# Expert gating in a PEER layer: one-hot columns interleaved in twos, and one weighting operation for two float16 parts

## The chip, the cores and the metric

The kernel runs on one NeuronCore of a Trainium2 chip. The metric is the device time of one execution in microseconds (us). The engines are named as in the profile: PE (TensorE, matmuls; its weight loads are listed apart as PEld), DVE (VectorE), ACT (ScalarE), POOL (GpSimd) and SP (SyncE, which issues most transfers).

## The reference, cut to what matters

A token sequence of 256 positions and width 1024 runs through two layers with mixers and feed-forward parts and then through a third, hybrid layer, whose feed-forward part is a PEER layer: 8 heads each choose 16 of 128 x 128 = 16384 experts for every token. This is the part that the change touches:

```python
PEER_HEADS = 8; PEER_NKEYS = 128; PEER_EXPERTS = 128 * 128; PEER_TOPK = 16
qh = (xc @ w_q).reshape(Ct, H, 2, PEER_QDIM // 2)
s = jnp.einsum("nhad,akd->nhak", qh, sub_keys).astype(f32)
top_s, top_i = lax.top_k(s, K)
...
best_s, pos = lax.top_k(cand, K)
eidx = jnp.take_along_axis(cand_idx, pos, axis=-1)      # 128 * i + j
gate = jax.nn.softmax(best_s, axis=-1)
ug = u_tab[eidx]
vg = v_tab[eidx]
hpre = jnp.einsum("nd,nhkd->nhk", xc, ug).astype(f32)
act = (gate * jax.nn.gelu(hpre, approximate=False)).astype(x.dtype)
return jnp.einsum("nhk,nhkd->nd", act, vg)
```

## The kernel before

All weights stream from memory in blocks of 128 x 1024 float32, each issued by SP. `Stream._split` (lines 247 and 248) turns a block into two fp32r parts: ACT writes the rounded part `hi`, DVE the remainder `lo`. Every dense product is then three matmuls (hi by x-high, hi by x-low, lo by x-high).

The PEER layer doesn't gather experts. It computes gelu(x u) for all 16384 of them, in two halves of 64 rows i (`u_phase`, matmuls of 256 columns at lines 330 to 332), into `H[0]` and `H[1]`, whose partition is j and whose free axes are i and the token t. Then it multiplies H by a dense table of gates that is zero where an expert wasn't chosen, and multiplies the result by all of v (the v phase, matmuls of 512 columns at line 1343).

`routing` (line 1410) leaves, for every token, 128 choices (8 heads x 16) on the partitions: `ri` and `rj` hold the two halves of the expert's number in bfloat16, `rg` the gate scaled by 2^15 as two float16 parts (the rounded value at line 1529, the remainder at line 1530).

`gates` (line 1533) builds the table from these. It takes eight tokens at a time, 32 groups for each half of H, 64 in all. A group is
- on DVE: `oj` (line 1545), which compares `rj` with 0 to 127 and gives a one-hot row of 128 columns for each token; `oi` (line 1546), the same for `ri` and the 64 rows of this half; `gi` (line 1549), `oi` times the gate, one operation for each of the two float16 parts;
- on PE (line 1555): for each token two matmuls, one for each part, with `oj` of the token as the weights (128 x 128) and `gi` of the token as the moving operand (128 x 64), summed over the 128 choices into one PSUM bank for the eight tokens;
- on DVE (line 1558), one group later: H times that bank.

The four tokens of a half group lie side by side in the innermost axis of `oj`, `oi` and `gi`, and `iota` holds each of its numbers four times for the comparison. A token's columns, as the matmul reads them, are thus every fourth float16 element.

The gating group is a generator: the kernel's `pump` advances it between the blocks of the main loop by a credit. The groups of `H[0]` run during the second half of the u phase, those of `H[1]` during the first half of the v phase. `oj` and `gi` have two buffers each, `oi` has one.

Of the kernel before, what the change touches and what calls it, by code (L numbers as in the profile page):

```python
# [12 lines left out]
BF16 = mybir.dt.bfloat16  # L13
F16 = mybir.dt.float16
# [3 lines left out]
ALU = mybir.AluOpType  # L18
# [3 lines left out]
P = 128  # L22
T = 256
# [110 lines left out]
def _constants():  # L134

    f = np.float32
    parts = []

    def put(name, a):
        a = np.asarray(a, f).reshape(P, -1)  # L140
        CON[name] = (sum(p.shape[1] for p in parts), a.shape[1])
        parts.append(a)

    i = np.arange(P)
    r, c = i[:, None], i[None, :]
    put("ident", np.eye(P))
    inv = (f(10000.0) ** (-np.arange(32, dtype=f) / f(32))).astype(f)
    ang = (np.arange(T, dtype=f)[:, None] * inv[None, :]).astype(f)
    put("cos", np.tile(np.cos(ang).T, (4, 1)))
    put("sin", np.tile(np.sin(ang).T, (4, 1)))  # L150
    put("causal", np.concatenate([np.zeros((P, P)), np.where(c <= r, 0, BIG)], axis=1))
    put("sb_m01", r < c)
    put("sb_add", np.concatenate([np.where(r < c, 0, -BIG), np.zeros((P, P)), np.where(r < c, 0, -BIG)], axis=1))
    put("sb_tri", np.where(r >= c, -1, 0))
    put("sb_one", -np.ones((P, P)))
    lev = [np.where(r > c, 1, 0), np.where(r <= c, 1, 0)]
    msk = []
    for m in (64, 32, 16, 8, 4, 2, 1):
        blk = c // (2 * m)
        last = blk * 2 * m + m - 1  # L160
        second = (c % (2 * m)) >= m
        lev.append(np.where(second, (r > last) & (r <= c), (r > c) & (r <= last)))
        msk.append((r // (2 * m) == c // (2 * m)) & (r % (2 * m) < m) & (c % (2 * m) >= m))
    msk.append(r == c)
    put("hg_lev", np.concatenate(lev, axis=1))
    put("hg_msk", np.concatenate(msk, axis=1))
    slopes = [2.0 ** -(h + 1) for h in range(8)]
    ali = []
    for s in slopes:
        ali += [s * (P + r - c), np.where(c <= r, s * (r - c), BIG)]  # L170
    put("alibi", np.concatenate(ali, axis=1))
    cmp = []
    for tt in range(2):
        for s in slopes:
            d = (tt * P + r) - (16 * np.arange(32)[None, :] + 31)
            cmp.append(np.where((d >= 0) & (np.arange(32)[None, :] < 15), s * d, BIG))
    put("cmp_bias", np.concatenate(cmp, axis=1))
    put("cmp_row", np.stack([i >= 31, i >= 0], axis=1))
    put("iota_j", np.broadcast_to(np.repeat(np.arange(P), 4), (P, 4 * P)))
    put("iota16", np.broadcast_to(np.repeat(np.arange(16), 16), (P, 256)))  # L180
    starts = []
    for a0, a1, w in CAND:
        base = sum((y - x) * z for x, y, z in CAND if y <= a0)
        starts += [base + (a - a0) * w for a in range(a0, a1)]
    put("starts", np.broadcast_to(np.repeat(starts, 16), (P, 256)))
    put("dstarts", np.broadcast_to(np.repeat(np.diff([0] + starts), 16), (P, 256)))
    return np.concatenate(parts, axis=1)


def _arrays(inp):  # L190
    names, blocks = [], []
    for n, b in _weights(inp):
        names.append(n)
        blocks.append(b)
    w = np.stack(blocks)
    x = inp["x"][0].reshape(T, NK, P).transpose(2, 1, 0)
    sk = inp["peer_sub_keys_2"][0].transpose(0, 2, 1).reshape(P, P)
    pe = np.tile(inp["nsa_cmp_pe_2"][0].T, (2, 1))
    wc = np.stack([inp["nsa_w_cmp_k_2"][0], inp["nsa_w_cmp_v_2"][0]]).reshape(2, 2, 16, 64, 64).transpose(1, 3, 0, 2, 4)
    wc = wc.reshape(P, -1)  # L200
    arrays = {
        "w": w, "x": x, "vec": _vectors(inp), "con": _constants(),
        "sk": sk, "pe": pe, "wc": wc, "fin": inp["norm_final_2"].reshape(1, D),
    }
    return names, {k: np.ascontiguousarray(v, dtype=np.float32) for k, v in arrays.items()}
# [54 lines left out]
class K:  # L260
# [498 lines left out]
    def hybrid(self, acc):  # L759
        nc, tc = self.nc, self.tc  # L760
        xh, xl = (lambda k: self.xh[:, k]), (lambda k: self.xl[:, k])
        with ExitStack() as c:
# [106 lines left out]
            def gates():  # L869
# [4 lines left out]
                for h in range(4):  # L874
                    nc.vector.tensor_scalar(hgg[:, h], hgg[:, h], self.vec("hgn", h), None, ALU.mult)

            self.later(gates, 1.5)
            fill(self.both(lambda q: self.hgrn(q, hq, hk, hf, hg_i, hgg, ob["hg"]),
                           lambda q: self.nsa(q, ns_q, ns_k, ns_c, ns_v, gate, ob["nsa"])))
# [375 lines left out]
    def peer(self, acc):  # L1255
        nc, tc = self.nc, self.tc
        mm = nc.tensor.matmul
        HALF = P // 2
        with ExitStack() as c:
            pk = c.enter_context(tc.tile_pool(name="pk", bufs=1, reuse_waits="tile"))  # L1260

            ri = pk.tile([P, T], BF16, name="ri")
            rj = pk.tile([P, T], BF16, name="rj")
            rg = pk.tile([P, 2, T], F16, name="rg")
            iota = pk.tile([P, P, 4], BF16, name="iota")
            o = CON["iota_j"][0]
            nc.gpsimd.dma_start(iota, self.a["con"][:, o:o + 4 * P].rearrange("p (j t) -> p j t", t=4))
            H = [None, None]
            hp0 = c.enter_context(tc.tile_pool(name="h0", bufs=1, reuse_waits="tile"))
            H[0] = hp0.tile([P, HALF, T], F32, name="H0")  # L1270
# [16 lines left out]
            with ExitStack() as c2:  # L1287
# [9 lines left out]
                g = self.vec("ffn2")  # L1297
# [112 lines left out]
    def routing(self, rp, qT, sk, ri, rj, rg):  # L1410
        nc, tc = self.nc, self.tc
        mm = nc.tensor.matmul
        with ExitStack() as c:
            p = c.enter_context(tc.tile_pool(name="ro", bufs=1, reuse_waits="tile"))

            def table(name):
                t = p.tile([P, 16, 16], BF16, name="t_" + name)
                o = CON[name][0]
                nc.gpsimd.dma_start(t, self.a["con"][:, o:o + 256].rearrange("p (a s) -> p a s", s=16))
                return t  # L1420

            starts, dstarts, iota = table("starts"), table("dstarts"), table("iota16")
            rest = p.tile([P, P], F32, name="rest")
            rest2 = p.tile([P, NCAND], F32, name="rest2")
            for tt in range(2):
# [3 lines left out]
                for h4 in range(2):  # L1429
                    bs = [self.bank() for _ in range(2)]  # L1430
                    for h in range(4):
                        for a in range(2):
                            mm(bs[a][:, h * P:(h + 1) * P], qT[64 * a:64 * a + 64, 4 * h4 + h, tt * P:(tt + 1) * P], sk[64 * a:64 * a + 64],
                               start=h == 0, stop=True, skip_group_check=True, tile_position=(64 * a, 0))
# [14 lines left out]
                o = 0  # L1449
                for a0, a1, w in CAND:  # L1450
                    n = a1 - a0
# [68 lines left out]
                b = self.bank()  # L1520
                for n, t in enumerate((key[:, 0], key[:, 1], best)):
                    nc.tensor.transpose(b[:, n * P:(n + 1) * P], t.rearrange("p h s -> p (h s)"), self.ident)
                ts = slice(tt * P, (tt + 1) * P)
# [2 lines left out]

                g = p.tile([P, P], F32, name="g")
                nc.vector.tensor_scalar(g, b[:, 2 * P:3 * P], GSCALE, None, ALU.mult)
                nc.vector.tensor_copy(rg[:, 0, ts], g)
                nc.vector.tensor_tensor(rg[:, 1, ts], g, rg[:, 0, ts], ALU.subtract)  # L1530
                yield 3.5

    def gates(self, pool, H, half, ri, rj, rg, iota):

        nc = self.nc
        HALF = P // 2
        prev = None
        for t8 in range(T // 8 + 1):
            if t8 < T // 8:
                ts = slice(8 * t8, 8 * t8 + 8)  # L1540
                oj = pool.tile([P, 2, P, 4], F16, name="oj")
                oi = pool.tile([P, 2, HALF, 4], F16, name="oi", bufs=1)
                gi = pool.tile([P, 2, 2, HALF, 4], F16, name="gi")
                r4 = lambda t: t.rearrange("p (g t) -> p g t", t=4)[:, :, None, :]
                nc.vector.tensor_tensor(oj, iota[:, None].to_broadcast([P, 2, P, 4]), r4(rj[:, ts]).to_broadcast([P, 2, P, 4]), ALU.is_equal)
                nc.vector.tensor_tensor(oi, iota[:, None, half * HALF:(half + 1) * HALF].to_broadcast([P, 2, HALF, 4]),
                                        r4(ri[:, ts]).to_broadcast([P, 2, HALF, 4]), ALU.is_equal)
                for n in range(2):
                    nc.vector.tensor_tensor(gi[:, n], oi, r4(rg[:, n, ts]).to_broadcast([P, 2, HALF, 4]), ALU.mult)
            yield 1.5  # L1550
            if t8 < T // 8:
                b = self.bank().rearrange("p (t i) -> p t i", t=8)
                for t in range(8):
                    for n in range(2):
                        nc.tensor.matmul(b[:, t], oj[:, t // 4, :, t % 4], gi[:, n, t // 4, :, t % 4], start=t + n == 0, stop=n == 1, skip_group_check=True)  # L1555
            if prev is not None:
                pb, pt = prev
                nc.vector.scalar_tensor_tensor(H[:, :, pt], pb.rearrange("p t i -> p i t"), 1.0 / GSCALE, H[:, :, pt], ALU.mult, ALU.mult)  # L1558
            prev = (b, ts) if t8 < T // 8 else None
            yield 0.6  # L1560
# [21 lines left out]
```

## Time and profile before

| what | us |
|---|---|
| median of three runs | 1740.42 (1740.07 to 1741.46) |
| the profiled execution's own time | 1740.35 |
| its span, from the first instruction to the last | 1738.6 |
| PE busy | 1721.9 |
| DVE busy | 1310.0 |
| ACT busy | 889.7 |
| PE busy in gating matmuls (line 1555), 1024 of them | 74.3 |

A time is read at three levels. The share of the span says which engine is busy longest. The chain of work that ended last says which instructions the end hangs on, and by how much each moves the end on (a matmul's recorded duration is longer than that, since matmuls overlap). The duration of a single instruction says what an engine is occupied with. Idle time of an engine that isn't waited for costs nothing.

### The profile page before, as it was taken

The page shows a single profiled execution, that of the slowest core. Times are in us where ns is not written, and L with a number is a line of the kernel's source. Part 1 is how long each engine was busy: PE and PEld are TensorE (multiplying, and loading weights), DVE is VectorE, ACT ScalarE, POOL GpSimd, SP SyncE. Part 2 cuts the span into 40 slices and gives each one's busy share as a digit, 9 for nine tenths or more (in the row PEclk, how much of TensorE's full clock was granted, in tenths as well). Part 3 has the DMA queues.
Part 4 walks back from the last instruction along what each step waited for, and adds up shares of the span by engine and source line. Part 5 has one row for each costly group of instructions (what it writes and reads, how often), then busy time and mean ns, then how long its engine had stood idle before and what let it go on. Part 6 is the DMA issues. An engine that isn't in the chain of part 4 may idle for free.

```text
span 1738.6 us, 33154 instructions
## 1 busy us (share of the span) xinstructions
PE 1721.9 (99%) x13299; PEld 1617.3 (93%) x13299; DVE 1310.0 (75%) x2532; ACT 889.7 (51%) x1322; POOL 27.6 (2%) x66
## 2 busy tenths in 40 slices
PE   8999999999999999999999999999999999999998
PEld 8999999979999998998799999999999888888886
DVE  7779976867997676868678989777776888855555
ACT  6466655556665547535657454433334343445443
POOL 0000000000000000100000000000000000000001
PEclk9999999999999999999999999999999999999999
DMA  7555565555565555633355464544445444455553
GB/s 240 188 178 179 184 203 183 185 154 161 180 194 186 181 170 168 208 122 94 99 188 194 146 207 160 192 151 154 152 152 170 161 166 158 159 180 188 190 193 120
DMA packets 87226, 297.25 MB, mean 171 GB/s; under 512 B 10784, under 2 KB 15680, under 8 KB 87072
## 3 DMA queue, kind: packets, MB, share of 16 engines
q1 hardware_dynamic: 84000, 288.92, 50.9%
q0 software_dynamic: 2640, 5.66, 1.3%
q8 instruction: 104, 1.70, 0.4%
q10 hardware_dynamic: 432, 0.56, 0.1%
q14 instruction: 50, 0.41, 0.1%
HBM read 292.03 MB, written 1.05 MB: 169 GB/s over the span
## 4 chain that ended last, share of the span: by engine, by line
PE 95%; DVE 1%; DMA 1%; ACT 1%; SPq 1%; issue 0%; DVEq 0%; ACTq 0%
PE bank L330 21%; PE bank L332 21%; PE bank L331 21%; PE bank L1343 20%; PE bank L1555 4%; PE bank L397 1%; PE bank L396 1%; PE bank L395 1%; PE bank L1223 1%; DMA raw<-in_w_dram 1%; SPq L666 1%; PE bank L1096 0%; PE bank L1118 0%; PE bank L1106 0%; ACT hi L247 0%
## 5 line engine op out<-in xcount | busy, mean ns | idle before, releaser
L247 ACT ACTIVATE hi<-raw 128x1024 fp32r<-128x1024 f32 (+2 forms) x552 | 573.6, 1046 | 714.8 <-PE bank L331 395.1
L248 DVE TENSOR_TENSOR lo<-raw,hi 128x1024 fp32r<-128x1024 f32 (+2 forms) x552 | 662.2, 1206 | 320.4 <-ACT hi L247 316.3
L330 PE MATMUL bank<-xh,hi 128*128 128x256 f32 x2624 | 748.0, 285 | 4.7 <-ACT hi L247 4.7
L331 PE MATMUL bank<-xl,hi 128*128 128x256 f32 x2624 | 743.2, 283 | 0.0
L332 PE MATMUL bank<-xh,lo 128*128 128x256 f32 x2624 | 742.1, 283 | 0.1
L330 PEld LDWEIGHTS bank<-xh,hi 128*128 128x128 f32 x2624 | 503.1, 192 | 8.4 <-ACT hi L247 4.9
L331 PEld LDWEIGHTS bank<-xl,hi 128*128 128x128 f32 x2624 | 502.9, 192 | 1.1 <-issue 0.9
L332 PEld LDWEIGHTS bank<-xh,lo 128*128 128x128 f32 x2624 | 502.4, 192 | 0.9 <-DVE lo L248 0.4
L1343 PE MATMUL bank<-hi,xh 128*128 128x512 f32 x512 | 161.7, 395 | 0.0
L1343 PE MATMUL bank<-hi,xl 128*128 128x512 f32 x512 | 159.0, 390 | 0.0
L1343 PE MATMUL bank<-lo,xh 128*128 128x512 f32 x512 | 158.9, 390 | 0.0
L1343 PEld LDWEIGHTS bank<-lo,xh 128*128 128x128 f32 x512 | 96.1, 188 | 20.7 <-DVE lo L248 0.3
L1343 PEld LDWEIGHTS bank<-hi,xl 128*128 128x128 f32 x512 | 96.1, 188 | 20.2
L1343 PEld LDWEIGHTS bank<-hi,xh 128*128 128x128 f32 x512 | 94.2, 189 | 17.5
L332 PE MATMUL bank<-ah,lo 128*128 128x256 f32 x352 | 98.9, 281 | 0.0
L330 PE MATMUL bank<-ah,hi 128*128 128x256 f32 x352 | 98.6, 280 | 0.0
L331 PE MATMUL bank<-al,hi 128*128 128x256 f32 x352 | 97.9, 278 | 0.0
L1558 DVE SCALAR_TENSOR_TENSOR H<-bank,H 128x512 f32<-128x512 f32 x64 | 44.0, 688 | 43.4 <-PE bank L1555 43.4
L1555 PE MATMUL bank<-gi,oj 128*128 128x64 f16 x1024 | 74.3, 241 | 0.0
L1555 PEld LDWEIGHTS <-oj 128*128 128x128 f16 x1024 | 62.8, 118 | 9.7 <-issue 4.2
L330 PEld LDWEIGHTS bank<-ah,hi 128*128 128x128 f32 x352 | 66.2, 188 | 0.0
L331 PEld LDWEIGHTS bank<-al,hi 128*128 128x128 f32 x352 | 66.2, 188 | 0.0
(385 smaller groups left out, 1823.5 us busy)
## 6 DMA issues: line engine op xcount, KB each, us to landing
raw<-in_w_dram SPq DMA_DIRECT2D x540, 512.0 KB, 3.3
x<-in_x_dram SPq DMA_DIRECT2D x8, 128.0 KB, 4.2
raw<-in_w_dram SPq DMA_DIRECT2D x8, 128.0 KB, 4.5
alibi<-in_con_dram POOLq DMA_DIRECT2D x8, 128.0 KB, 3.0
raw<-in_w_dram SPq DMA_DIRECT2D x4, 256.0 KB, 4.3
q<-t SPq DMA_DIRECT2D x32, 32.0 KB, 3.6
k<-t SPq DMA_DIRECT2D x32, 32.0 KB, 1.9
wc<-in_wc_dram POOLq DMA_DIRECT2D x2, 512.0 KB, 4.5
```

The costliest lines, as they stand in the source:

```text
L247: nc.scalar.activation(hi[:, c], raw[:, c], AF.Copy)
L248: nc.vector.tensor_tensor(lo[:, c], raw[:, c], hi[:, c].bitcast(F32), ALU.subtract)
L330: mm(out, wh, xh, start=start, stop=False, skip_group_check=True)
L331: mm(out, wh, xl, start=False, stop=False, skip_group_check=True)
L332: mm(out, wl, xh, start=False, stop=stop, skip_group_check=True)
L395: mm(o, xh(k)[:, ts], hi[:, c], start=k == 0, stop=False, skip_group_check=True)
L396: mm(o, xl(k)[:, ts], hi[:, c], start=False, stop=False, skip_group_check=True)
L397: mm(o, xh(k)[:, ts], lo[:, c], start=False, stop=k == NK - 1, skip_group_check=True)
L666: nc.sync.dma_start(dst[o:o + 32, 2 * a + r // 2], t1[32 * r:32 * r + 32, x])
L1343: nc.tensor.matmul(acc[tt][n], x[:, s, tt * P:(tt + 1) * P], w[u][:, n * 512:(n + 1) * 512], start=i == 0 and x is self.xh and u == 0, sto ...
L1555: nc.tensor.matmul(b[:, t], oj[:, t // 4, :, t % 4], gi[:, n, t // 4, :, t % 4], start=t + n == 0, stop=n == 1, skip_group_check=True)
L1558: nc.vector.scalar_tensor_tensor(H[:, :, pt], pb.rearrange("p t i -> p i t"), 1.0 / GSCALE, H[:, :, pt], ALU.mult, ALU.mult)
```

## The change

The tokens of a group lie side by side in twos and no longer in fours, so that a token's columns are every second float16 element. `rg` gets the layout [token group of 8, part, token], so that the two parts can be read by one operation, which weights `oi` for both parts at once. `iota` holds each number twice.

```diff
-    put("iota_j", np.broadcast_to(np.repeat(np.arange(P), 4), (P, 4 * P)))
+    put("iota_j", np.broadcast_to(np.repeat(np.arange(P), 2), (P, 2 * P)))
...
-            rg = pk.tile([P, 2, T], F16, name="rg")
-            iota = pk.tile([P, P, 4], BF16, name="iota")
+            rg = pk.tile([P, T // 8, 2, 8], F16, name="rg")
+            iota = pk.tile([P, P, 2], BF16, name="iota")
...
-                nc.vector.tensor_copy(rg[:, 0, ts], g)
-                nc.vector.tensor_tensor(rg[:, 1, ts], g, rg[:, 0, ts], ALU.subtract)
+                gt = g.rearrange("p (a t) -> p a t", t=8)
+                gs = slice(16 * tt, 16 * tt + 16)
+                nc.vector.tensor_copy(rg[:, gs, 0], gt)
+                nc.vector.tensor_tensor(rg[:, gs, 1], gt, rg[:, gs, 0], ALU.subtract)
...
-                oj = pool.tile([P, 2, P, 4], F16, name="oj")
-                oi = pool.tile([P, 2, HALF, 4], F16, name="oi", bufs=1)
-                gi = pool.tile([P, 2, 2, HALF, 4], F16, name="gi")
-                r4 = lambda t: t.rearrange("p (g t) -> p g t", t=4)[:, :, None, :]
-                nc.vector.tensor_tensor(oj, iota[:, None].to_broadcast([P, 2, P, 4]), r4(rj[:, ts]).to_broadcast([P, 2, P, 4]), ALU.is_equal)
-                nc.vector.tensor_tensor(oi, iota[:, None, half * HALF:(half + 1) * HALF].to_broadcast([P, 2, HALF, 4]),
-                                        r4(ri[:, ts]).to_broadcast([P, 2, HALF, 4]), ALU.is_equal)
-                for n in range(2):
-                    nc.vector.tensor_tensor(gi[:, n], oi, r4(rg[:, n, ts]).to_broadcast([P, 2, HALF, 4]), ALU.mult)
+                oj = pool.tile([P, 4, P, 2], F16, name="oj")
+                oi = pool.tile([P, 4, HALF, 2], F16, name="oi", bufs=1)
+                gi = pool.tile([P, 2, 4, HALF, 2], F16, name="gi")
+                r2 = lambda t: t.rearrange("p (g t) -> p g t", t=2)[:, :, None, :]
+                nc.vector.tensor_tensor(oj, iota[:, None].to_broadcast([P, 4, P, 2]), r2(rj[:, ts]).to_broadcast([P, 4, P, 2]), ALU.is_equal)
+                nc.vector.tensor_tensor(oi, iota[:, None, half * HALF:(half + 1) * HALF].to_broadcast([P, 4, HALF, 2]),
+                                        r2(ri[:, ts]).to_broadcast([P, 4, HALF, 2]), ALU.is_equal)
+                rgp = rg[:, t8].rearrange("p n (g t) -> p n g t", t=2)[:, :, :, None, :]
+                nc.vector.tensor_tensor(gi, oi[:, None].to_broadcast([P, 2, 4, HALF, 2]), rgp.to_broadcast([P, 2, 4, HALF, 2]), ALU.mult)
...
-                        nc.tensor.matmul(b[:, t], oj[:, t // 4, :, t % 4], gi[:, n, t // 4, :, t % 4], start=t + n == 0, stop=n == 1, skip_group_check=True)
+                        nc.tensor.matmul(b[:, t], oj[:, t // 2, :, t % 2], gi[:, n, t // 2, :, t % 2], start=t + n == 0, stop=n == 1, skip_group_check=True)
```

No instruction moves; the place on which a term rests is DVE's work for the first gating groups of `H[0]`. Before the change it stands there in this order (`lo` is the split of a weight block; numbers tell the buffers apart, so that `oj_14060` and `oj_14084` belong to two groups):

```order
L1545 TENSOR_TENSOR oj_14060<-iota_11239,rj_11237 128x1024
L1546 TENSOR_TENSOR oi_14061<-iota_11239,ri_11236 128x512
L1545 TENSOR_TENSOR oj_14084<-iota_11239,rj_11237 128x1024
L248 TENSOR_TENSOR lo_13905<-raw_13798,hi_13904 128x1024
L1549 TENSOR_TENSOR gi_14062<-oi_14061,rg_11238 128x512 x2
L1546 TENSOR_TENSOR oi_14085<-iota_11239,ri_11236 128x512
L1549 TENSOR_TENSOR gi_14086<-oi_14085,rg_11238 128x512 x2
L248 TENSOR_TENSOR lo_13936<-raw_13830,hi_13935 128x1024
```

Each group's `gi` is two operations of 512 elements, one behind the other. DVE at the same place after the change (the lines are numbered a little further, and the second group's buffers one lower):

```order
L1548 TENSOR_TENSOR oj_14060<-iota_11239,rj_11237 128x1024
L1549 TENSOR_TENSOR oi_14061<-iota_11239,ri_11236 128x512
L1548 TENSOR_TENSOR oj_14083<-iota_11239,rj_11237 128x1024
L248 TENSOR_TENSOR lo_13905<-raw_13798,hi_13904 128x1024
L1552 TENSOR_TENSOR gi_14062<-oi_14061,rg_11238 128x1024
L1549 TENSOR_TENSOR oi_14084<-iota_11239,ri_11236 128x512
L1552 TENSOR_TENSOR gi_14085<-oi_14084,rg_11238 128x1024
L248 TENSOR_TENSOR lo_13936<-raw_13830,hi_13935 128x1024
```

The two weightings of 512 elements have become one of 1024 in their place, and everything around them stands where it stood; the order on PE, ACT and SP is the same as before.

## Rows read from the trace of the kernel before

**Rows 1.** The page's first lines: span; busy us, share and instructions by engine.

```profile
span 1738.6 us, 33154 instructions
## 1 busy us (share of the span) xinstructions
PE 1721.9 (99%) x13299; PEld 1617.3 (93%) x13299; DVE 1310.0 (75%) x2532; ACT 889.7 (51%) x1322; POOL 27.6 (2%) x66
```

**Rows 2.** The page's chain that ended last, shares of the span by engine.

```profile
PE 95%; DVE 1%; DMA 1%; ACT 1%; SPq 1%; issue 0%; DVEq 0%; ACTq 0%
```

**Rows 3.** Busy time by stretch: length, engines (instructions), granted clock, DMA share, GB/s.

```profile
1130.00:1305.00 175.00, 175.00 (x1673) 173.75 (x1672) 127.48 (x195) 65.68 (x76) 0.00 (x0) 1.00 0.46 152
...
1347.00:1532.00 185.00, 185.00 (x1177) 152.45 (x1176) 153.05 (x235) 73.01 (x84) 0.54 (x1) 1.00 0.49 161
```

**Rows 4.** The chain in order of time, in U: start us, us, what.

```profile
1128.70 0.12 PE bank L330
1130.49 0.99 PE bank L1555 x16
1131.49 0.17 PE bank L330
1137.29 1.00 PE bank L1555 x16
```

**Rows 5.** The chain in order of time, in V.

```profile
1355.50 2.82 PE bank L1343 x12
1358.32 1.00 PE bank L1555 x16
```

**Rows 6.** The chain in order of time, in the v phase behind the gating.

```profile
1539.87 20.17 PE bank L1343 x89
```

**Rows 7.** The chain in order of time: short fp32 matmuls of 15, 64, 1 columns.

```profile
747.59 1.97 PE bank L1041 x64
...
775.81 1.73 PE bank L1061 x16
...
809.66 1.68 PE bank L443 x16
```

**Rows 8.** Weight loads by line: duration ns minimum/median/maximum, first and last start, forms.

```profile
L1555 PEld LDWEIGHTS <-oj x1024: 112/118/137, 1130.3 to 1529.1; 128*128 128x128 f16 x171
...
L1041 PEld LDWEIGHTS bank<-xpe,wc x128: 132/138/138, 747.5 to 769.5; 128*64 128x64 f32 x128
...
L443 PEld LDWEIGHTS bank<-ones,ssum x20: 188/192/192, 18.2 to 929.7; 128*128 128x128 f32 x20
```

**Rows 9.** DVE by line in the same form; last lo in V (busy, mean, idle before).

```profile
L1545 DVE TENSOR_TENSOR oj<-iota,rj x64: 678/683/687, 1116.1 to 1520.5; 128x1024 f16<-128x1024 bf16 x64
...
L1546 DVE TENSOR_TENSOR oi<-iota,ri x64: 414/424/429, 1116.7 to 1517.1; 128x512 f16<-128x512 bf16 x64
...
L1549 DVE TENSOR_TENSOR gi<-oi,rg x128: 415/418/425, 1118.8 to 1521.4; 128x512 f16<-128x512 f16 x128
...
L1558 DVE SCALAR_TENSOR_TENSOR H<-bank,H x64: 682/688/693, 1131.6 to 1530.2; 128x512 f32<-128x512 f32 x64
...
L248 DVE TENSOR_TENSOR lo<-raw,hi 128x1024 fp32r<-128x1024 f32 x56 | 68.6, 1225 | 30.3 <-ACT hi L247 28.7
```

**Rows 10.** DVE in order of time, one group in U: start us, us, instruction, idle before.

```profile
1131.60 0.69 DVE L1558 SCALAR_TENSOR_TENSOR H<-bank,H 128x512 f32<-128x512 f32 x1 [1.75 <-PE bank L1555]
1132.21 1.22 DVE L248 TENSOR_TENSOR lo<-raw,hi 128x1024 fp32r<-128x1024 f32 x1
1133.34 0.68 DVE L1545 TENSOR_TENSOR oj<-iota,rj 128x1024 f16<-128x1024 bf16 x1
1133.94 0.75 DVE L1549 TENSOR_TENSOR gi<-oi,rg 128x512 f16<-128x512 f16 x2
1134.73 0.42 DVE L1546 TENSOR_TENSOR oi<-iota,ri 128x512 f16<-128x512 bf16 x1
```

**Rows 11.** The two operations that write rg, by line.

```profile
L1529 DVE CAST rg<-g x2: 216/218/220, 1030.8 to 1115.6; 128x128 f16<-128x128 f32 x2
...
L1530 DVE TENSOR_TENSOR rg<-g,rg x2: 292/292/293, 1031.1 to 1115.9; 128x128 f16<-128x128 f32 x2
```

More of the change, by code (lines that the diff above doesn't have):

```diff
@@ L1263, in peer @@
             rj = pk.tile([P, T], BF16, name="rj")
-            rg = pk.tile([P, 2, T], F16, name="rg")
-            iota = pk.tile([P, P, 4], BF16, name="iota")
+            rg = pk.tile([P, T // 8, 2, 8], F16, name="rg")
+            iota = pk.tile([P, P, 2], BF16, name="iota")
             o = CON["iota_j"][0]
-            nc.gpsimd.dma_start(iota, self.a["con"][:, o:o + 4 * P].rearrange("p (j t) -> p j t", t=4))
+            nc.gpsimd.dma_start(iota, self.a["con"][:, o:o + 2 * P].rearrange("p (j t) -> p j t", t=2))
             H = [None, None]
```

## The prediction

> **What bounds the kernel now.** I read the share of each engine first: PE is busy for 1721.9 us of a span of 1738.6 us [rows 1]. The chain of work that ended last says the same from the other end: 95% of it is PE, and DVE has 1% [rows 2]. So I then looked at the two stretches in which the gating code runs, by engine. The first (U, the second half of the u phase) goes from 1130 to 1305 us and the second (V, the first half of the v phase) from 1347 to 1532 us. [...] What the change is worth in time is therefore read from PE's own instructions, and DVE's work counts only if it grows until PE waits for it.
>
> The chain in order of time gives PE's price without the pipeline's overlap. A 256-column fp32r matmul advances the chain by 0.12 us. A group of 16 gating matmuls advances it by 0.99 us, and the matmul behind it takes 0.17 us, 0.05 us more than usual [rows 4]. In V a group takes 1.00 us [rows 5]. That is 62 ns for a matmul of only 64 columns, and 64 groups x 1.04 us = 67 us of the whole time.
>
> **What 64 columns should cost.** From the rows: 89 matmuls of 512 columns take 20.17 us [rows 6], 227 ns each; 256 columns take 120 ns. The difference, 107 ns for 256 columns, is 0.417 ns a column, and 120 - 256 x 0.417 leaves 13 ns that does not depend on columns. So 64 columns read at that rate would take 27 + 13 = 40 ns. The gating matmul takes 22 ns more. What is different about it: both its operands are float16, its columns are read from every fourth element (8 bytes apart), and it is short.
>
> Shortness alone isn't the reason: 64 matmuls of 15 columns, each with its own weight load of 64 columns, take 1.97 us, 31 ns each [rows 7]. Nor does the load look like the limit. With fp32 weights it is: 16 matmuls of 64 columns take 1.73 us and 16 of one column take 1.68 us, so some 107 ns whatever the columns [rows 7]. But the float16 load is recorded at 118 ns, the 64-column fp32 load at 138 ns and the 128-column one at 192 ns [rows 8]; at (192 - 138) / 64 = 0.84 ns a column the float16 load is worth about 40 columns, some 34 ns, and a load runs beside the matmul before it (the 107 ns load is covered by a 120 ns matmul). That leaves the moving operand: 64 columns at 8 bytes take about as long as 118 columns side by side would ((62 - 13) / 0.417). I take it that the step between columns slows that read.
>
> **The change, part by part.**
> (a) Columns 4 bytes apart, not 8, in both operands of all 1024 gating matmuls. PE's instructions and their order are the same. If the step is what costs, a half step brings the read back towards 27 ns, the load (34 ns) still fits beside it, and the period falls from 62 to 40 ns: 16 x 22 ns = 0.35 us a group, 64 x 0.35 = 22.4 us. The bounds: nothing (no row shows a 4-byte step), and 62 - 31 = 31 ns x 1024 = 31.7 us if it came down to the shortest pair in the trace [rows 7]. A loss on PE has no row that suggests it, since the reads only move closer. I take 40 ns, since it is the rate that 512- and 256-column matmuls both keep, and PE is the bound in both stretches, so that the whole of it shows. I leave the 0.05 us behind each group as it is.
>
> [...] The 62 ns against 40 ns [rows 5, 6] speak for a loss somewhere in these reads, but no run so far shows a second step to compare.
>
> (b) One weighting operation of 1024 elements in place of two of 512. The two take 418 ns each; the comparison for oj, of 1024 float16 elements, takes 683 ns [rows 9]. In order of time the pair holds DVE for 0.79 us (1133.94 to 1134.73) and oj for 0.60 us (1133.34 to 1133.94) [rows 10]. So DVE gains some 0.19 us a group, 12 us in all, and none of it on the path: PE is 100% busy beside it. The matmuls wait for both halves before and after, so their data comes no later.
>
> (c) The comparisons oj and oi keep their counts; their innermost run shrinks from 4 to 2 elements. No row has a run of 2 with these types. Bounds: the same 683 and 424 ns, or the rate of an operation that handles one element at a time, 1225 ns for 1024 and 688 ns for 512 (H) [rows 9]. I take the same: a pair of adjacent float16 elements is still there in every operand. [...] The other end is the rival below.
>
> (d) rg is written in 16 runs of 8 elements, by a copy of 218 ns and a subtraction of 292 ns, twice each [rows 11]. Were they twice as long, that is 1 us of DVE time in all; the last of them ends at 1116 us and the first gating matmul starts at 1130 us, so 14 us hide it. The table iota is half as large and is loaded long before. Both at nothing.
>
> Sum: the profiled execution took 1740.35 us (span 1738.6 and 1.75 around it), 0.07 us under the median of the three runs. 1740.35 - 22.4 = 1718.0 us.
>
> **The rivals.**
> (1) No change. The step costs nothing, and 62 ns is what a float16 load and its matmul need in this form, for instance one after the other: 34 + 27 ns = 61 ns. For it: the sum fits as well as mine. Against it: the other shapes overlap load and matmul. DVE's gain is hidden, so 1740 us (1738 to 1742).
> (2) A part of it. Load-bound: the fp32 load's 105 ns [rows 7] halved for elements of half the size is 53 ns; then the period falls only from 62 to about 53 ns, 9 us, 1731 us (1727 to 1736).
> (3) Slower: DVE loses its doubled rate with runs of 2 and becomes the bound in V. Price a group: oj 1225 - 683 = 542 ns, oi 688 - 424 = 264 ns, weighting 1225 - 750 = 475 ns (the pair takes 0.75 us [rows 10]), together 1.28 us. V holds 30 groups (60 weightings); DVE has 185 - 153 = 32 us to spare [rows 3], 1.07 us a group, and that is the point from which it decides. Then V needs at least 153 + 38 = 191 us, and some of DVE's idle time before lo (30.3 us, nearly all for ACT's hi [rows 9]) stays as well: 6 to 25 us. With no gain on PE that is 1746 to 1765, about 1752 us. U would still fit (127 + 29 x 1.28 = 164 of 175 us). For it speaks only that no row shows a run of 2.
>
> **How the numbers follow.** Forecast 0.42, rival (1) 0.32, rival (2) 0.18, rival (3) 0.08. A measurement of this kernel can tell about 0.2%, 3.5 us, from no change. Faster by more than that: the forecast and rival (2), 0.60; within it 0.32; slower 0.08. Predicted is the forecast's 1718. Its own range is 1713 to 1725 (a period of 35 to 47 ns). Both signs don't hold most of the chance, but no change holds too much to be left out, so the range goes from 1713 to 1741; outside are rival (3), the upper edge of rival (1) and a period near 31 ns.
>
> **What would show it.** Right: in the chain, a gating group of 16 at about 0.64 us in place of 0.99, PE still busy for all of U and V, and U and V each some 11 us shorter for the same matmuls. Rival (1): 0.99 us again. Rival (2): 0.85 us. Rival (3): oj at 1.2 us and PE waiting for DVE ahead of the gating loads. For (b): one weighting at about 683 ns, DVE busy for some 10 us less in all (128 x 418 - 64 x 683 ns). The prediction is wrong if the group keeps its length, or if PE stands idle where it doesn't now.

## The result and the profile after

The changed kernel takes 1710.83 us (median of 4 runs, 1710.46 to 1711.75), the kernel before 1740.3 us: a ratio of 0.983, 95% interval 0.9813 to 0.9847, 29.5 us less. It is faster, as forecast, by more than the 22.4 us of the forecast, and 2.2 us below the lower end of the range.

The page's first lines of the changed kernel, which answer to [rows 1]:

```profile
span 1708.7 us, 33092 instructions
## 1 busy us (share of the span) xinstructions
PE 1690.9 (99%) x13299; PEld 1587.4 (93%) x13299; DVE 1302.5 (76%) x2468; ACT 889.4 (52%) x1322; POOL 27.5 (2%) x66
```

PE has the same 13299 matmuls and is busy 31.0 us less; DVE has 64 instructions fewer. Both are as full as before, in share: PE is still the bound, and the span shrank by what PE's work shrank. Two stretches with gating, in U and in the v phase, which answer to [rows 3]:

```profile
1130.00:1305.00 175.00, 175.00 (x1822) 173.62 (x1821) 135.57 (x180) 70.97 (x82) 0.00 (x0) 1.00 0.50 164
1336.00:1500.00 164.00, 164.00 (x1140) 132.91 (x1139) 144.03 (x201) 71.37 (x81) 0.53 (x1) 1.00 0.53 175
```

PE is busy for all of both, at a granted clock of 1.00 as before, so the clock has no part in the gain.

The chain in order of time (start us, us, what), first in U and then in V, which answers to [rows 4, 5]; the gating matmul is line 1558 now:

```profile
1131.37 0.50 PE bank L1558 x16
1131.87 0.20 PE bank L330
1137.70 0.49 PE bank L1558 x16
...
1343.04 0.50 PE bank L1558 x16
1343.54 5.53 PE bank L1343 x24
```

A gating group takes 0.50 us where it took 0.99 to 1.00 [rows 4, 5]: 31 ns a matmul in place of 62. The matmul behind a group takes 0.20 us where it took 0.17. Over 64 groups that is some 32 us less and 1.9 us more, some 30 us.

Where it went by stage: the first gating load, the first matmul of the v phase and the last gating load started at 1130.3, 1345.1 and 1529.1 us before. The first and the last of these stand in [rows 8]; the v phase's, by line, of the kernel before (duration in ns minimum/median/maximum, first and last start in us, forms):

```profile
L1343 PE MATMUL bank<-hi,xh x512: 387/389/476, 1345.1 to 1729.2; 128*128 128x512 f32 x171
```

The same by line after:

```profile
L1558 PEld LDWEIGHTS <-oj x1024: 95/97/102, 1131.2 to 1499.2; 128*128 128x128 f16 x171
L1558 PE MATMUL bank<-gi,oj x1024: 191/193/204, 1131.2 to 1499.3; 128*128 128x64 f16 x171
...
L1343 PE MATMUL bank<-hi,xh x512: 388/389/477, 1330.8 to 1699.4; 128*128 128x512 f32 x171
```

So the stretch from the first gating load to the v phase went from 214.8 to 199.6 us, the gating in the v phase from 184.0 to 168.4 us, 30.8 us in all. What lies before took 0.9 us longer, in PE work that the change leaves as it was (in the runs below this first start lies anywhere from 1129.9 to 1131.5 us), and 30.8 - 0.9 us is what the span lost. The recorded load of the weights went from 118 ns [rows 8] to 97 ns.

DVE by line in the same form, which answers to [rows 9, 11]:

```profile
L1548 DVE TENSOR_TENSOR oj<-iota,rj x64: 678/683/687, 1116.5 to 1492.0; 128x1024 f16<-128x1024 bf16 x64
L1549 DVE TENSOR_TENSOR oi<-iota,ri x64: 412/424/428, 1117.1 to 1488.9; 128x512 f16<-128x512 bf16 x64
L1552 DVE TENSOR_TENSOR gi<-oi,rg x64: 680/683/693, 1119.3 to 1492.6; 128x1024 f16<-128x1024 f16 x64
...
L1531 DVE CAST rg<-g x2: 220/220/220, 1030.7 to 1116.1; 128x128 f16<-128x128 f32 x2
L1532 DVE TENSOR_TENSOR rg<-g,rg x2: 291/292/293, 1030.9 to 1116.3; 128x128 f16<-128x128 f32 x2
```

The comparisons cost what they cost before, 683 and 424 ns, with runs of two elements as with runs of four, and the merged weighting costs what oj costs. Writing rg in the new layout costs nothing more.

### The profile page after: what moved, and what is told of

It reads as the page before. It is cut to its first block, busy times and chain, and to the rows that moved or that the text cites. A ratio compares the mean times of both kernels' runs of the same rounds, so it can differ in the third digit from the quotient of the medians.

```text
span 1708.7 us, 33092 instructions
## 1 busy us (share of the span) xinstructions
PE 1690.9 (99%) x13299; PEld 1587.4 (93%) x13299; DVE 1302.5 (76%) x2468; ACT 889.4 (52%) x1322; POOL 27.5 (2%) x66
## 4 chain that ended last, share of the span: by engine, by line
PE 97%; DVE 1%; ACT 1%; SPq 1%; issue 0%; DMA 0%; DVEq 0%; ACTq 0%
PE bank L330 22%; PE bank L331 22%; PE bank L332 22%; PE bank L1343 20%; PE bank L1558 2%; PE bank L1223 1%; PE bank L397 1%; PE bank L396 1%; PE bank L395 1%; SPq L666 1%; PE bank L1096 1%; PE bank L1118 0%; PE bank L1106 0%; PE bank L477 0%; PE bank L693 0%
## 5 line engine op out<-in xcount | busy, mean ns | idle before, releaser
L332 PEld LDWEIGHTS bank<-ah,lo 128*128 128x128 f32 x352 | 66.1, 188 | 0.0
L596 ACT ACTIVATE y<-e,taps 128x256 f32<-128x256 f32 x88 | 38.6, 497 | 18.8 <-DVE e L587 18.8
```

What stands on the lines that cost most here:

```text
L332: mm(out, wl, xh, start=False, stop=stop, skip_group_check=True)
L596: nc.scalar.activation(y[:, a], e[:, a, 2:], AF.Copy, scale=w[2])
```

## The experiments

The theory to test: the gain is PE's alone, and within PE it is the step between the columns of the moving operand. Rivals: the step between the columns of the weights, or DVE's merged operation. In the names below w is the step of the weights and m that of the moving operand, in float16 elements; w4m4 has the steps of the kernel before, w2m2 is the changed kernel. Those with other steps change nothing but the addresses that one line reads, in the changed kernel; each of them was timed in one execution. Executions of the kernel before, 13 of them beside these runs, lie within 1.5 us of each other, so differences of that size in time are not read.

**The two parts of the change, one at a time.** The merged weighting (and rg's layout, which it needs) without the new step:

```diff
-                for n in range(2):
-                    nc.vector.tensor_tensor(gi[:, n], oi, r4(rg[:, n, ts]).to_broadcast([P, 2, HALF, 4]), ALU.mult)
+                rgp = rg[:, t8].rearrange("p n (g t) -> p n g t", t=4)[:, :, :, None, :]
+                nc.vector.tensor_tensor(gi, oi[:, None].to_broadcast([P, 2, 2, HALF, 4]), rgp.to_broadcast([P, 2, 2, HALF, 4]), ALU.mult)
```

> The kernel before with the merged weighting alone: columns stay 8 bytes apart, rg gets the new layout, one operation of 1024 elements replaces two of 512. My theory (all of the gain is PE's read of the columns): 1740 us, no change, with a gating group at 0.99 us in the chain and DVE busy some 10 us less in all. Rival (DVE's shorter work brings the matmuls forward and part of the 29.5 us is DVE's): 1735 us or less with the group still at 0.99 us.

And the new step with two weightings:

```diff
-                nc.vector.tensor_tensor(gi, oi[:, None].to_broadcast([P, 2, 4, HALF, 2]), rgp.to_broadcast([P, 2, 4, HALF, 2]), ALU.mult)
+                for n in range(2):
+                    nc.vector.tensor_tensor(gi[:, n], oi, rgp[:, n].to_broadcast([P, 4, HALF, 2]), ALU.mult)
```

> The changed kernel with two weightings of 512 elements again, so that only the step of the columns differs from the kernel before. My theory: 1711 us, as the changed kernel, group at 0.50 us. Rival (the merged operation is part of the gain): 1714 us or more.

The merged weighting alone takes 1740.87 us beside 1740.94 us of the kernel before (ratio 0.9999, 0.999 to 1.0009). The new step alone takes 1709.5 us (ratio 0.9822, 0.9806 to 0.9838). The page's busy times of the kernel without the new step:

```profile
PE 1722.3 (99%) x13299; PEld 1618.0 (93%) x13299; DVE 1306.1 (75%) x2468; ACT 890.1 (51%) x1322; POOL 27.6 (2%) x66
```

A gating group in its chain, then one in the chain of the kernel with the new step and two weightings, then that kernel's gating load by line:

```profile
1348.24 1.00 PE bank L1557 x16
```

```profile
1338.54 0.50 PE bank L1559 x16
```

```profile
L1559 PEld LDWEIGHTS <-oj x1024: 96/97/102, 1130.0 to 1498.1; 128*128 128x128 f16 x171
```

All of the gain belongs to the step. DVE's 64 instructions fewer bring nothing, since PE is busy for all of the gating stretches [rows 3] and doesn't wait for DVE. The two kernels with the new step differ by 1.3 us, but not in the gating: from its first to its last load it takes 368.1 us here and 368.0 us in the changed kernel. The first of these loads comes 1.2 us earlier here (1130.0 and 1131.2 us), behind work that is the same in both. I don't count it for or against the merged operation.

**Which operand.**

```diff
-nc.tensor.matmul(b[:, t], oj[:, t // 2, :, t % 2], gi[:, n, t // 2, :, t % 2], ...
+nc.tensor.matmul(b[:, t], oj[:, t // 4 * 2:t // 4 * 2 + 2].rearrange("p g (j e) f -> p (g j) (e f)", e=2)[:, :, t % 4], gi[:, n, t // 2, :, t % 2], ...
```

> The changed kernel, but the matmuls read the weights oj in steps of 4 elements (8 bytes) from the same tile, the moving operand gi in steps of 2 as it is; DVE's work is untouched, only the address pattern of the weight load changes, so the table of gates is no longer that of the reference. Theory M (the moving operand's step set the 62 ns): a group stays near 0.50 us, 1711 us. Theory W (the weight load's step set it): 0.99 us a group and 1740 us. Recorded load: 97 ns if the step costs loads nothing, 118 ns if it does.

```diff
-nc.tensor.matmul(b[:, t], oj[:, t // 2, :, t % 2], gi[:, n, t // 2, :, t % 2], ...
+nc.tensor.matmul(b[:, t], oj[:, t // 2, :, t % 2], gi[:, n, t // 4 * 2:t // 4 * 2 + 2].rearrange("p g (j e) f -> p (g j) (e f)", e=2)[:, :, t % 4], ...
```

> The changed kernel, but the matmuls read the moving operand gi in steps of 4 elements (8 bytes), the weights oj in steps of 2 as they are; only that address pattern changes, so the table of gates is no longer that of the reference. Theory M: 0.99 us a group and 1740 us. Theory W: 0.50 us a group and 1711 us. If each operand has a part, both this and the opposite mix lie between, or the slower of the two sets the group.

w4m2 took 1713.88 us, w2m4 1738.77 us. A group in the chain in V and the gating load by line, first of w4m2, then of w2m4:

```profile
1340.42 0.56 PE bank L1558 x16
```

```profile
L1558 PEld LDWEIGHTS <-oj x1024: 112/116/133, 1129.9 to 1502.6; 128*128 128x128 f16 x171
```

```profile
1347.52 0.98 PE bank L1558 x16
```

```profile
L1558 PEld LDWEIGHTS <-oj x1024: 96/117/118, 1131.0 to 1527.5; 128*128 128x128 f16 x171
```

Theory M holds. The wide step of the moving operand alone gives nearly the whole 0.99 us back, that of the weights alone 0.06 us a group. The two hardly add up: 0.48 and 0.06 us on top of 0.50 would be 1.04, and 0.99 to 1.00 were measured with both wide, so the slower of the two reads nearly sets the pace alone. The recorded load doesn't tell which is slower: it is 116 to 117 ns in both, also where the load itself reads in steps of 2. So a load is recorded longer also when only the matmul beside it reads in wide steps (the longer matmul alone doesn't do it: beside matmuls of 60 ns in steps of 2, in cols128 below, it is 97 ns).

**How the cost goes with the step.** Three more steps of the moving operand; of each, only its address in that line changes (steps of 1, 3 and 8 in this order):

```diff
+gi[:, n, t // 2].rearrange("p j e -> p (j e)")[:, 64 * (t % 2):64 * (t % 2) + 64]
+gi[:, n].rearrange("p g j f -> p (g j f)")[:, 2 * t:2 * t + 192].rearrange("p (j e) -> p j e", e=3)[:, :, t % 2]
+gi[:, n].rearrange("p g (j e) f -> p (g j) (e f)", e=4)[:, :, t]
```

> The changed kernel, but the moving operand's 64 columns are read side by side (step 1, 2 bytes) from the same tile, weights in steps of 2; so the table of gates is no longer that of the reference. It asks whether the 31 ns a matmul that the changed kernel has left still hang on the step. If they do (the read costs by the bytes it spans all the way down): 15 to 20 ns, 0.3 us a group, some 1698 us. If a floor is reached (64 columns at 0.42 ns are 27 ns, or the weight load): 31 ns, 0.50 us a group, 1711 us.

> The changed kernel, but the moving operand is read in steps of 3 elements (6 bytes), weights in steps of 2; so the table of gates is no longer that of the reference. Theory S (the read's cost goes with the bytes that it spans: 59 ns for 512 bytes at a step of 4): 384 bytes, some 45 ns, 0.72 us a group, 1725 us. Theory E (beyond 4 bytes each element costs an access of its own, 0.93 ns): 59 ns, 0.95 us a group, 1737 us. [...]

> The changed kernel, but the moving operand is read in steps of 8 elements (16 bytes), weights in steps of 2; so the table of gates is no longer that of the reference. Theory S: 1024 bytes spanned, some 118 ns a matmul, 1.9 us a group, 1800 us. Theory E: 59 ns as at a step of 4, 0.95 us a group, 1737 us.

They took 1709.38, 1726.15 and 1794.38 us. The chain, one group of each, in the order 1, 3, 8:

```profile
1338.63 0.48 PE bank L1558 x16
```

```profile
1341.27 0.77 PE bank L1558 x16
```

```profile
1337.00 1.87 PE bank L1558 x16
```

| step of the moving operand | bytes from column to column | bytes spanned by 64 columns | group of 16, us | ns a matmul |
|---|---|---|---|---|
| 1 | 2 | 128 | 0.48 | 30 |
| 2 | 4 | 256 | 0.50 | 31 |
| 3 | 6 | 384 | 0.77 | 48 |
| 4 | 8 | 512 | 0.98 | 61 |
| 8 | 16 | 1024 | 1.87 | 117 |

From a step of 2 on the cost goes with the bytes spanned: (61 - 31) / 256 = 0.12 and (117 - 61) / 512 = 0.11 ns a byte. Theory S holds, E is out by step 8, where it gave 59 ns. Below a step of 2 there is next to nothing to win: half the bytes take 30 ns, near the 27 ns of 64 columns at 0.42 ns, so there it is no longer the bytes that cost. At a step of 2 the two costs meet: a column at 0.42 ns, and its 4 bytes at 0.11 ns a byte, 0.44 ns. No run had a step wider than 8; how the cost goes on beyond is not shown.

For 64 columns, a step of 8 bytes costs twice the time of a step of 4 bytes (61 against 31 ns), and 6 bytes cost half as much again (48 ns).

**Length, step and load apart.** The matmuls cut in two, once in steps of 2 and once in steps of 4 for the moving operand:

```diff
-nc.tensor.matmul(b[:, t], oj[:, t // 2, :, t % 2], gi[:, n, t // 2, :, t % 2], ...
+for i in (0, 32):
+    nc.tensor.matmul(b[:, t, i:i + 32], oj[:, t // 2, :, t % 2], gi[:, n, t // 2, i:i + 32, t % 2], ...
```

For steps of 4, the moving operand in the last line is instead:

```diff
+gi[:, n, t // 4 * 2 + i // 32, :, :].rearrange("p (j e) f -> p j (e f)", e=2)[:, :, t % 4]
```

> The changed kernel with every gating matmul cut into two of 32 columns, each with its own load of the same 128 columns of weights: 2048 loads and matmuls in place of 1024. If the 31 ns a matmul are the columns (27 ns and some 4): 13 + 4 = 17 ns each, 0.55 us a group of 32, 1714 us. If they are the weight load: 31 ns each, 1.0 us a group, 1742 us.

> The changed kernel with every gating matmul cut into two of 32 columns that are read in steps of 4 elements (8 bytes), weights in steps of 2; so the table of gates is no longer that of the reference. Theory S (the moving read costs by the bytes it spans, 0.11 ns a byte): 256 bytes, some 31 ns each, 1.0 us a group of 32, 1740 us, against 25.5 ns each at a step of 2. Rival (the wide step costs a fixed amount a matmul, 59 - 31 = 28 ns): 25 + 28 = 53 ns each, 1.7 us a group, 1785 us.

They took 1731.25 and 1747.68 us. One group of 32 in the chain of each:

```profile
1343.57 0.81 PE bank L1559 x32
```

```profile
1131.03 1.07 PE bank L1559 x32
```

Half the columns in steps of 2 take 25 ns, neither the 17 ns of the columns nor the 31 ns of a bound by the load. These 25 ns are the shortest of a float16 load and its matmul in these runs, and 64 columns, at 30 to 31 ns, lie just above them. In steps of 4 they take 33 ns, close to the 31 ns of theory S and far from 53: the wide step costs by the bytes spanned and not a fixed 28 ns a matmul.

The opposite, one matmul of 128 columns for both parts of a token:

```diff
-                    for n in range(2):
-                        nc.tensor.matmul(b[:, t], oj[:, t // 2, :, t % 2], gi[:, n, t // 2, :, t % 2], ...
+                    nc.tensor.matmul(b[:, t // 2 * 2:t // 2 * 2 + 2], oj[:, t // 2, :, t % 2], gi[:, :, t // 2, :, t % 2], ...
```

> The changed kernel with one gating matmul of 128 columns for each token, both float16 parts side by side, in place of two of 64: half as many loads and matmuls. It writes the parts of two tokens over the same 128 PSUM columns, so the table of gates is no longer that of the reference; DVE's work is untouched. It measures what does not depend on columns. My corrected theory (0.42 ns a column and 3 ns): 56 ns each, 0.45 us a group of 8, 1708 us. The prediction's term (13 ns fixed, as in the fp32r matmuls): 66 ns each, 0.53 us a group, 1713 us.

It took 1707.34 us. A group of eight in the chain and the load:

```profile
1341.30 0.48 PE bank L1557 x8
```

```profile
L1557 PEld LDWEIGHTS <-oj x512: 96/97/102, 1131.1 to 1496.1; 128*128 128x128 f16 x171
```

That is 60 ns for 128 columns and, from the changed kernel, 31 ns for 64: 0.45 ns a column and 2 ns that don't depend on columns. (128 columns in steps of 2 also span 512 bytes, which cost 61 ns in w2m4, so at this step the columns and the bytes ask for the same time.) My corrected 3 ns was near; the prediction's 13 ns is not there. Leaving out half of all loads saves 0.02 us a group, so the loads are hidden.

**The step of the weights, further.** As w4m2, with steps of 8:

```diff
+oj.rearrange("p g (j e) f -> p (g j) (e f)", e=4)[:, :, t]
```

> The changed kernel, but the weights are read in steps of 8 elements (16 bytes), the moving operand in steps of 2 as it is; so the table of gates is no longer that of the reference. Weights in steps of 4 gave 35 ns a matmul. If the load pays for the bytes that it spans as four reads of 32 columns side by side (512 bytes each, 0.11 ns a byte): some 58 to 62 ns, 0.95 us a group, 1738 us. If as one read of 2048 bytes: some 230 ns, 3.7 us a group, 1920 us. If the step costs the load little at all: 38 ns, 0.6 us a group, 1716 us.

It took 1744.09 us. The chain and the load:

```profile
1350.20 1.00 PE bank L1558 x16
```

```profile
L1558 PEld LDWEIGHTS <-oj x1024: 141/171/174, 1131.5 to 1532.7; 128*128 128x128 f16 x171
```

Steps of 2, 4 and 8 give 31, 35 and 62 ns (the first of these is set by the moving operand). From 4 to 8 the 128 columns span 1024 bytes more and cost 27 ns more, 0.027 ns a byte: a quarter of what the moving operand pays. The 62 ns agree with the first of the three values above; its four reads side by side were my assumption, and how the load reads its columns is not shown. One read of 2048 bytes at the moving operand's rate, 230 ns, is out.

## Why the prediction was right and where it failed

- **The bound, and where to read the price.** Right. PE's busy time fell by 31.0 us and the span by 29.9 us; U and the gating in the v phase are shorter by 15.2 and 15.6 us.
- **That the step costs, and that it is the moving operand's.** Right, and the reason was the one given: the load was too short to fill 62 ns, and the columns took longer than columns side by side. w2m4 and w4m2 show it. That its 34 ns for the load lie next to w4m2's 35 ns is luck: they were worked out from a recorded duration, and the same working makes 87 ns of w8m2's 171 ns, where 62 ns were measured.
- **The size: 40 ns a matmul.** This is the step that failed. The prediction took 120 ns for 256 fp32r columns and 227 ns for 512, drew a line through them, and carried its 13 ns for zero columns over to a float16 matmul of 64. Here these 13 ns are a third of the result. Measured are 31 ns, and cols128 gives 2 ns at zero columns. With 2 ns in place of 13, the prediction's own sum would have been 29 ns, near the 31; but the trace before had no row for it, as all its other matmuls are fp32 or fp32r. A period of 31 ns stood in the trace before, as the shortest pair of a load and a matmul (64 matmuls of 15 columns in 1.97 us [rows 7]); the prediction named them as the outer bound, then set its range to end at 35 ns, and put a period near 31 ns outside. By its own row the bound was attainable, and the range should have held it. That bound and the result agree in size but not in cause: cols32 shows that a pair with a float16 load can go at 25 ns, and w2m1 that half the bytes still take 30 ns, so what holds 64 columns at 31 ns is the columns.
- **The 0.05 us behind each group.** Taken as unchanged, it grew to 0.08 us: 64 x 0.03 = 1.9 us that the sum didn't have. The paragraph behind this list has the reason.
- **(b) one weighting.** Right that it brings nothing: one_weighting is at 0.9999. DVE's busy time fell by 3.9 us there (and by 7.5 us in the changed kernel), not by 10: the sum 128 x 418 - 64 x 683 ns counts durations whose ends overlap, while busy time counts the pair as 0.75 us [rows 10] against 0.68 us. What the other 3.6 us in the changed kernel are stays open.
- **(c) runs of two, (d) rg's layout.** Right: 683, 424, 220 and 292 ns. That a pair of adjacent elements is enough was an assumption that no row before showed. The doubled rate of rival (3) is, as measured, 683 ns for the 1024 float16 elements of oj where lo, 1024 elements in fp32, takes 1225 ns [rows 9]; how many elements DVE handles at a time is not shown. Rival (3) is out: oj keeps its 683 ns, and PE is busy throughout.
- **Rivals (1) and (2).** Out: the group is at 0.50 us, not at 0.99 or 0.85. A load and its matmul don't go one after the other either: cols128 saves half the loads and gains 0.02 us a group.

The delay behind a group fits a wait for the fp32r matmul's own load, which would hide under the last gating matmul: behind matmuls of 48 ns (w2m3, first line) the fp32r matmul takes 0.18 us, behind 117 ns (w2m8, last two lines) the usual 0.12 us.

```profile
1132.23 0.18 PE bank L330
...
1344.62 1.87 PE bank L1558 x16
1346.49 0.12 PE bank L330
```

The last gating matmul and the delay come to some 110 ns each time (62 + 50, 48 + 60, 31 + 80), near the 107 ns of an fp32 load [rows 7], and 117 ns cover it.

What the 13 ns of the fp32r matmuls are wasn't tried. The law of the moving operand (0.11 ns a byte) gives 113 ns for their 1024 bytes and 225 ns for 2048, near the measured 120 and 227 ns. They may be bound by that read too; no run here separates it from their columns.

Left of the gating after the change are 0.50 + 0.08 us a group, 37 us. Step 1 would save 0.02 us a group more, but its layout would leave DVE's comparisons without adjacent tokens; what they then take is not shown.

## What to carry to other kernels

If a matmul's operand is interleaved with others, look at the bytes from column to column: here 2-byte columns 4 bytes apart were read at nearly the rate of columns side by side (64 of them in 31 and 30 ns), and from there on, up to 16 bytes apart, the moving operand's read cost 0.11 to 0.12 ns for each byte it spanned. The weights' cost a quarter of that between 8 and 16 bytes (0.027 ns). Price a short matmul by the chain's advance for a group divided by its count, and don't extend a line through long matmuls of another type to it: its intercept becomes the result. And a floor that another row shows to be attainable belongs into the range.

## What was unexpected

- The moving operand's 2-byte columns are read at nearly the full rate only up to 4 bytes apart: 30 ns at a step of 2 bytes, 31 at 4, 48 at 6, 61 at 8, 117 at 16, for 64 columns.
- The weights are four times less sensitive, byte for byte (0.027 against 0.11 ns from 8 to 16 bytes): load and matmul take 31, 35 and 62 ns at steps of 4, 8 and 16 bytes.
- A weight load's recorded duration changes with the step of the matmul beside it (97 ns at a step of 2, 117 ns at 4, w2m4, where the load's own step is 2) and so doesn't say which read is slow.
- A pair of a load and a matmul of 32 float16 columns takes 25 ns.
